# A hybrid decoder layer: the output projection as seven half-size products instead of a full product

## The chip, the cores and the metric

One core of one Trainium2 chip runs the kernel. The metric is the device time of one execution in microseconds (us); three runs of the kernel before took 1262.02, 1262.72 and 1263.93, with a median of 1262.72.

## The reference, cut to what is computed

One layer over 1024 tokens of width 1024, all in float32:

```python
h = rmsnorm(x, norm_g)
proj = h @ w_in                       # q, k, v, gates, decay code, merge logits
...
y_a = o_gla @ w_pa                    # o_gla: chunked gated linear attention (4 heads)
y_b = o_sb @ w_pb                     # o_sb: stick-breaking attention (8 heads)
gates = sigmoid(m_logits + b_gate)
merged = gates[:, :, 0] * y_a + gates[:, :, 1] * y_b
x = x + merged @ w_o                  # 1024 x 1024 by 1024 x 1024
return rmsnorm(x, final_g)
```

The change concerns the last two lines: `merged @ w_o`, the residual and the final norm, and also the places where their operands are prepared.

## The kernel before

Every float32 operand of a product is held as two parts: a high part that ScalarE (ACT) rounds off, and a low part, the difference, that VectorE (DVE) computes (`split`, L152 to 154). A product of two such operands is three matmuls: high by high, high by low and low by high. Tokens are halved (n = 0, 1 with 512 tokens each) and the rows of a weight are taken as even and odd blocks of 128 (`kb % 2`), so an activation such as `mq[n, e]` is a "quarter": 128 partitions, 4 blocks, 512 tokens.

The stages in time: the norm of x and its transposes (eight token blocks, about the first 40 us); the decay code of the linear attention, with sums of quarters of h on GpSimd (POOL); the input projection, whose products are made by `pair_job` (L233) with seven half-size products in place of eight; the two attentions; the w_pa and then the w_pb product; and the output projection.

In the w_pb stage, `m_half` (L988 on) takes each product of 512 tokens, loads the gate `d_gb` and the other branch `d_ma` into a staging tile `o`, forms the merged value and splits it into its quarter of `mq`. `Line` is the helper that issues these units beside the products. Some DMA queues matter: SP issues almost all DMAs, in program order, and one that waits holds all behind it. The engine orders are made by a scheduler, except inside `manual_schedule`, where ACT and DVE run in the order in which the code is written.

In the output projection (L1003 to L1048), the first 256 columns of w_o (`wsA`) are multiplied for all eight token blocks first, with the residual columns in `xA`; meanwhile the other 768 columns are loaded and split (`wB`). Then each token block has one bank of 512 columns and one of 256. `finish` adds the residual (DVE), squares with a running sum (ACT, `ssq`) and multiplies with the final norm's weight `fg` (DVE). When all three column parts of a block are in, DVE makes `pre` and `r`, POOL raises `r` to the power -1/2, and DVE and ACT scale the row; SP and ACT store it. `raw` (two buffers) and `tt` (one buffer) are 4 KB-a-partition staging tiles for loaded weights; `ev` holds the tiles `f`.

Of the kernel before, what the change touches and what calls it, by code (L numbers as in the profile page):

```python
# [94 lines left out]
def hybrid_layer(ctx: ExitStack, tc: tile.TileContext, x, norm_g, w_in, w_up, b_dec,  # L95
# [30 lines left out]
    d_ogl = dram_set("ogl", GLA_H, [P, 2, T])  # L126
    d_ga, d_gb, d_ma = (dram_set(nm, KB, [P, T]) for nm in ("ga", "gb", "ma"))
    d_a21 = dram_set("a21", 2, [P, 4, HALF])

    ident = const.tile([P, P], F32, tag="ident", name="ident")  # L130
    make_identity(nc, ident)
# [8 lines left out]
    nhalf = const.tile([P, 1], F32, tag="nhalf", name="nhalf")  # L140
# [11 lines left out]
    def split(src, hi, lo, eng=nc.vector):  # L152
        nc.scalar.activation(hi, src, AF.Copy)  # L153
        eng.tensor_sub(lo, src, hi.bitcast(F32))  # L154
# [42 lines left out]
    def proj_n(ws, quads, tb, n=DV):  # L197

        pt = ps.tile([P, HALF], F32, tag="pp", name="pp", bufs=3)
        cs = slice(tb % 4 * P, (tb % 4 + 1) * P)  # L200
        for kb in range(KB):
            q = quads[tb // 4, kb % 2]
            h_, l_ = q[0][:, kb // 2, cs], q[1][:, kb // 2, cs]
            whi, wlo = ws(kb)
            nc.tensor.matmul(pt[:, 0:n], h_, whi, start=kb == 0, stop=False)  # L205
            nc.tensor.matmul(pt[:, 0:n], h_, wlo, start=False, stop=False)  # L206
            nc.tensor.matmul(pt[:, 0:n], l_, whi, start=False, stop=kb == KB - 1)  # L207
# [311 lines left out]
    f = {}  # L519
# [11 lines left out]
    def part(nm, j):  # L531
# [17 lines left out]
    manual = ExitStack()  # L549
# [3 lines left out]
    st.run(1)  # L553
    for i, s in enumerate("hl"):
        nc.sync.dma_start(d_a21[i], hq[1, 0][i].bitcast(F32))
    for fn, hs in ((code, ((0,), (1,))), (logit, ((0, 1), (2, 3))), (decay_a, ((0, 1), (2, 3))),
                   (decay_b, ((0,), (1,), (2,), (3,))), (decay_c, ((0,), (1,), (2,), (3,))),
                   (decay_d, ((0,), (1,), (2,), (3,))), (decay_e, ((0, 1, 2, 3),))):
        for group in hs:
            for h in group:  # L560
                fn(h)
            st.run(1)
    for ops in line:
        for op in ops:
            op()
        st.run(1)
# [214 lines left out]
    a21b = ctx.enter_context(tc.tile_pool(name="a21b", bufs=1, side="right", reuse_waits="tile"))  # L781
# [173 lines left out]


    pq = ctx.enter_context(tc.tile_pool(name="pq", bufs=1, reuse_waits="tile"))
    pb_ctx = ExitStack()
# [5 lines left out]
    mq = {}  # L964
# [19 lines left out]
    reload_split(bq, 3, 3)  # L984
    pb_load(1)[0]()
    st.run()
    mq.update(quads_in(a21b, "m"))

    def m_half(pt, eb, n):
        o = stage().bitcast(F32)  # L990
        nc.sync.dma_start(o[:, 0], d_gb[eb][:, half(n)])
        nc.sync.dma_start(o[:, 1], d_ma[eb][:, half(n)])
        nc.vector.tensor_mul(o[:, 0], pt, o[:, 0])
        nc.vector.tensor_add(o[:, 0], o[:, 0], o[:, 1])
        q = mq[n, eb % 2]
        split(o[:, 0], q[0][:, eb // 2], q[1][:, eb // 2])

    line = []
    for eb in range(KB):
        line += ([pb_load(eb + 2)] if eb + 2 < KB else []) + [pb_unit(eb, 0), pb_unit(eb, 1)]  # L1000
    Line(line).run()

    wsA = rows_of(load_w256(w_o, 0))  # L1003
    fg = pq.tile([P, D], F32, tag="fg", name="fg", bufs=1)
    nc.sync.dma_start(fg, final_g.partition_broadcast(P))
    xA = pq.tile([P, NT, DV], F32, tag="xA", name="xA", bufs=1)
    nc.sync.dma_start(xA, x2[:, 0:DV].rearrange("(b p) c -> p b c", p=P))
    ssq = pq.tile([P, NT, 3], F32, tag="ssq", name="ssq", bufs=1)
    pb_ctx.close()
    po = ctx.enter_context(tc.tile_pool(name="po", bufs=2, side="right", reuse_waits="tile"))  # L1010
    wB = [[po.tile([P, D - DV], F32R, tag=f"wo{s}{k}", name=f"wo{s}{k}", bufs=1) for k in range(KB)]
          for s in "hl"]
    ygA = po.tile([P, NT, DV], F32, tag="ygA", name="ygA", bufs=1)
    for kb in range(KB):
        raw = raw_tile().rearrange("p a b -> p (a b)")[:, 0:D - DV]
        nc.sync.dma_start(raw, w_o[kb * P:(kb + 1) * P, DV:D])
        split(raw, wB[0][kb], wB[1][kb])

    def finish(tb, k, c0, pt, y, yg):

        n = y.shape[-1]
        nc.vector.tensor_add(y, pt, y)
        junk = ps.tile([P, HALF], F32, tag="tr", name="junk")
        nc.scalar.activation(junk[:, 0:n], y, AF.Square, accum_out=ssq[:, tb, k:k + 1])
        nc.vector.tensor_mul(yg, y, fg[:, c0:c0 + n])

    for tb in range(NT):
        finish(tb, 0, 0, proj_n(wsA, mq, tb), xA[:, tb], ygA[:, tb])
    for tb in range(NT):
        ts = slice(tb * P, (tb + 1) * P)  # L1030
        y = po.tile([P, D - DV], F32, tag="y", name="y")
        nc.sync.dma_start(y, x2[ts, DV:D])
        yg = po.tile([P, D], F32, tag="yg", name="yg")
        nc.gpsimd.tensor_copy(yg[:, 0:DV], ygA[:, tb])
        for k, (c0, n) in ((1, (DV, HALF)), (2, (DV + HALF, DV))):
            a = c0 - DV
            pt = proj_n(lambda kb: (wB[0][kb][:, a:a + n], wB[1][kb][:, a:a + n]), mq, tb, n)
            finish(tb, k, c0, pt, y[:, a:a + n], yg[:, c0:c0 + n])
        pre = po.tile([P, 1], F32, tag="pre", name="pre")
        nc.vector.tensor_scalar(pre, ssq[:, tb, 0:1], ssq[:, tb, 1:2], D * EPS, op0=ALU.add, op1=ALU.add)  # L1040
        r = po.tile([P, 1], F32, tag="r", name="r")
        nc.vector.tensor_scalar(r, ssq[:, tb, 2:3], pre, 1.0 / D, op0=ALU.add, op1=ALU.mult)
        nc.gpsimd.tensor_tensor(r, r, nhalf, op=ALU.pow)
        cut = 640
        nc.vector.tensor_scalar(yg[:, 0:cut], yg[:, 0:cut], r, None, op0=ALU.mult)
        nc.sync.dma_start(o2[ts, 0:cut], yg[:, 0:cut])
        nc.scalar.activation(yg[:, cut:D], yg[:, cut:D], AF.Copy, scale=r)
        nc.scalar.dma_start(o2[ts, cut:D], yg[:, cut:D])  # L1048


_INS = ["x", "norm_g", "w_in", "w_dec_up", "b_dec", "gla_norm_g", "w_pa", "w_pb", "b_gate",
# [20 lines left out]
```

## Time and profile before

| | us |
|---|---|
| median of three runs | 1262.72 |
| the profiled execution, its own time | 1259.98 |
| its span, from the first to the last instruction | 1258.3 |
| TensorE busy | 1234.0 |
| VectorE (DVE) busy | 753.4 |
| ScalarE (ACT) busy | 519.8 |
| GpSimd (POOL) busy | 243.3 |

The profile is one execution, recorded instruction by instruction. PE is TensorE, SP the engine that issues DMAs; "SPq" marks a DMA issue, with the time that the issue took. A row of the timeline gives the start in us from the span's start, the duration, the engine, the line of the kernel, the operation, out<-in and, in brackets, how long the engine stood idle before it and what ended that. A row of groups gives a count, busy time and mean ns of one, and then idle time before them with its releasers. Rows of windows give the length, then the busy time of PE, weight loads, DVE, ACT and POOL with their counts, the granted clock, the share of the DMA engines and the GB/s. Matmuls are pipelined: the time of one is the distance between two starts, not the printed duration.

### The profile page before, as it was taken

Reading aid. Unit: us, or ns where it says so; the run is one execution under the profiler, and the core shown is the slowest. Engines: PE = TensorE matmul, PEld = TensorE weight load, DVE = VectorE, ACT = ScalarE, POOL = GpSimd, SP = SyncE. Lnnn points to the kernel's source line nnn. Section 1 sums busy time; section 2 is a strip of 40 time slices with the busy share of each in tenths; the row PEclk is TensorE's granted clock in tenths of the full one; section 3 lists DMA queues with packets and bytes.
Section 4 is the critical chain, followed back from the end, with each engine's and each line's share of the span. In section 5 each row is a group of like instructions: output and inputs, shape, how many; then the busy total and the mean of one; then the engine's idle time right before and its main releaser. Section 6 shows DMA issues by size and latency. Waiting matters only on the chain.

```text
span 1258.3 us, 18805 instructions
## 1 busy us (share of the span) xinstructions
PE 1234.0 (98%) x6947; PEld 1054.5 (84%) x6947; DVE 753.4 (60%) x1309; ACT 519.8 (41%) x1024; POOL 243.3 (19%) x280
## 2 busy tenths in 40 slices
PE   8999999999999999999999999999999999999998
PEld 8999999888888888888888877777777878888986
DVE  5682454545667666666564357778887775444533
ACT  5454332344344444444444444545644443122322
POOL 2400471323223233232323010000100000000010
PEclk9999999999999999999999999999999999999999
DMA  7547353534644565655433765444775437543232
GB/s 270 186 142 269 126 181 133 188 116 149 192 157 137 188 208 173 215 179 177 159 117 121 246 206 160 135 163 147 220 245 175 135 109 265 190 161 110 85 116 92
DMA packets 176982, 212.09 MB, mean 169 GB/s; under 512 B 11222, under 2 KB 129004, under 8 KB 174332
## 3 DMA queue, kind: packets, MB, share of 16 engines
q1 hardware_dynamic: 175740, 209.34, 50.8%
q10 hardware_dynamic: 1152, 1.57, 0.3%
q8 instruction: 54, 0.88, 0.3%
q14 instruction: 36, 0.29, 0.1%
HBM read 133.28 MB, written 77.59 MB: 168 GB/s over the span
## 4 chain that ended last, share of the span: by engine, by line
PE 84%; DVE 8%; DMA 3%; ACT 2%; issue 2%; SPq 0%; POOL 0%; DVEq 0%; POOLq 0%; ACTq 0%
PE pp L254 12%; PE pp L256 12%; PE pp L255 12%; PE pp L207 7%; PE pp L205 7%; PE pp L206 7%; PE pp L193 6%; PE pp L194 6%; PE pp L192 5%; DVE eb L828 3%; PE av L864 1%; DVE be L833 1%; PE tr L847 1%; PE av L865 1%; PE av L863 1%
## 5 line engine op out<-in xcount | busy, mean ns | idle before, releaser
L153 ACT ACTIVATE wh<-raw 128x1024 fp32r<-128x1024 f32 x57 | 60.4, 1060 | 125.8 <-PE pp L193 69.6
L154 DVE TENSOR_TENSOR wl<-tt,wh 128x1024 fp32r<-128x1024 f32 x48 | 58.8, 1224 | 69.3 <-ACT wh L153 69.1
L291 DVE TENSOR_TENSOR f<-pp,f 128x512 f32<-128x512 f32 x72 | 49.7, 690 | 81.2 <-PE pp L256 77.9
L154 DVE TENSOR_TENSOR wl<-raw,wh 128x1024 fp32r<-128x1024 f32 x57 | 78.2, 1371 | 29.4 <-ACT wh L153 28.4
L153 ACT ACTIVATE wh<-tt 128x1024 fp32r<-128x1024 f32 x48 | 50.9, 1061 | 75.7 <-PE pp L255 69.0
L830 POOL TENSOR_SCALAR_AFFINE_SELECT be<-be 128x128 f32<-128x128 f32 x64 | 23.0, 360 | 277.1 <-ACT be L822 211.1
L828 DVE TENSOR_TENSOR_SCAN eb<-eb 128x128 f32<-128x128 f32 (+6 forms) x56 | 71.8, 1282 | 5.6 <-ACT eb L821 3.1
L154 DVE TENSOR_TENSOR o<-pp,o 128x256 fp32r<-128x256 f32 (+1 forms) x72 | 32.4, 451 | 66.1 <-ACT o L153 63.0
L153 ACT ACTIVATE o<-pp 128x256 fp32r<-128x256 f32 (+1 forms) x72 | 29.0, 403 | 93.5 <-PE pp L207 90.3
L821 ACT ACTIVATE eb<-z 128x384 f32<-128x384 f32 (+4 forms) x96 | 48.4, 506 | 44.6 <-PE z L819 30.7
L260 ACT ACTIVATE f<-pp 128x512 f32<-128x512 f32 x72 | 42.5, 590 | 55.8 <-PE pp L256 55.8
L228 POOL TENSOR_TENSOR tt<-raw 128x512 f32<-128x512 f32 x24 | 31.2, 1302 | 150.4 <-DVE wl L154 135.8
L153 ACT ACTIVATE ath<-tr 128x512 fp32r<-128x512 f32 (+2 forms) x96 | 44.0, 496 | 38.8 <-PE tr L847 37.9
L215 POOL TENSOR_TENSOR r<-r,nhalf 128x1 f32<-128x1 f32 x40 | 23.4, 586 | 188.3 <-DVE r L214 188.3
L154 DVE TENSOR_TENSOR atl<-tr,ath 128x512 fp32r<-128x512 f32 (+2 forms) x96 | 51.1, 546 | 5.3 <-ACT ath L153 5.3
L864 PE MATMUL av<-atl,v 128*128 128x256 f32 x160 | 47.0, 293 | 3.9 <-DVE atl L154 3.9
L847 PE MATMUL tr<-ident,be 128*128 128x128 f32 x288 | 44.5, 278 | 5.8 <-DVE be L833 4.9
L847 PEld LDWEIGHTS tr<-ident,be 128*128 128x128 f32 x288 | 32.5, 140 | 20.7 <-DVE be L833 11.2
L192 PE MATMUL pp<-bh,wh 128*128 128x512 f32 x128 | 49.9, 390 | 0.0
L193 PE MATMUL pp<-bl,wh 128*128 128x512 f32 x128 | 49.9, 390 | 0.0
L194 PE MATMUL pp<-bh,wl 128*128 128x512 f32 x128 | 49.9, 390 | 0.0
L833 DVE TENSOR_TENSOR be<-be,eb 128x128 f32<-128x128 f32 (+3 forms) x64 | 48.3, 755 | 1.9
(406 smaller groups left out, 4177.2 us busy)
## 6 DMA issues: line engine op xcount, KB each, us to landing
raw<-in_w_in_dram SPq DMA_DIRECT2D x31, 1024.0 KB, 5.9
d_v<-o SPq DMA_DIRECT2D x32, 256.0 KB, 3.2
d_gv<-o SPq DMA_DIRECT2D x16, 512.0 KB, 2.7
v<-d_gv SPq DMA_DIRECT2D x32, 256.0 KB, 3.1
d_q<-o SPq DMA_DIRECT2D x16, 512.0 KB, 5.7
d_k<-o SPq DMA_DIRECT2D x16, 512.0 KB, 3.9
k<-d_k SPq DMA_DIRECT2D x8, 1024.0 KB, 5.0
v<-d_v SPq DMA_DIRECT2D x8, 1024.0 KB, 6.6
```

The costliest lines, as they stand in the source:

```text
L153: nc.scalar.activation(hi, src, AF.Copy)
L154: eng.tensor_sub(lo, src, hi.bitcast(F32))
L192: nc.tensor.matmul(pt, whi[:, kb], h_, start=kb == 0, stop=False)
L193: nc.tensor.matmul(pt, whi[:, kb], l_, start=False, stop=False)
L194: nc.tensor.matmul(pt, wlo[:, kb], h_, start=False, stop=kb == KB - 1)
L205: nc.tensor.matmul(pt[:, 0:n], h_, whi, start=kb == 0, stop=False)
L206: nc.tensor.matmul(pt[:, 0:n], h_, wlo, start=False, stop=False)
L254: nc.tensor.matmul(pt, bh[:, j], ah[:, j], start=first and j == 0, stop=False, skip_group_check=True)
L255: nc.tensor.matmul(pt, bh[:, j], al[:, j], start=False, stop=False, skip_group_check=True)
L256: nc.tensor.matmul(pt, bl[:, j], ah[:, j], start=False, stop=j == 3, skip_group_check=True)
L828: nc.vector.tensor_tensor_scan(rest, rest, rest, om[:, T - P:T - P + 1], op0=ALU.mult, op1=ALU.min)
L847: nc.tensor.transpose(pt[:, b * P:(b + 1) * P], be[:, c:c + P], ident)
```

## The change

The output projection becomes 28 products: seven half-size products u = 0 to 6, each for four blocks t of 128 tokens of either half. Sums of quarters of w_o (T1 to T4) and of the merged activation (S1 to S4) are formed on POOL, and written to DRAM until they are read back and split.

```
T1 = w12 - w11   T2 = w22 - T1   T3 = w22 - w12   T4 = w21 - T2
S1 = m21 + m22   S2 = S1 - m11   S4 = m12 - S2    S3 = m11 - m21
```

Here the first index of m is the token half and the second the even or odd row blocks; the first of w (`b[e][J]` in the code) is the even or odd row blocks and the second the column half. So product u has the operands (A11, B11), (A12, B21), (S2, T2), (S1, T1), (S4, B22), (S3, T3), (A22, T4). Two products at most share a bank of PSUM: u = 0, 2, 5 and 6 accumulate in the four banks `xb`; u = 1 has a `pp` bank of its own; u = 3 has a `pp` bank in which u = 4 goes on.

The early sums of w_o: four jobs load 1 MB each into `tt`, take four sums and store four times, spread over the units of the decay section.

```diff
+    def t_load(j):
+        wt[j] = sw.tile([P, 4, 4, P], F32, tag="tt", name="tt", bufs=1).rearrange("p q a c -> p q (a c)")
+        for two in range(2):
+            nc.sync.dma_start(wt[j][:, 2 * two:2 * two + 2],
+                              w_o[(2 * j + two) * P:(2 * j + two + 1) * P].rearrange("p (h c) -> p h c", h=2))
+    def t_sums(j):
+        a = wt[j]
+        for dst, x1, x2_ in ((0, 1, 0), (1, 3, 1), (3, 3, 0), (2, 2, 3)):
+            nc.gpsimd.tensor_sub(a[:, dst], a[:, x1], a[:, x2_])
+    def t_store(j):
+        for i, nm in enumerate(("T1", "T3", "T4", "T2")):
+            nc.sync.dma_start(d_t[nm][j // 2][:, j % 2], wt[j][:, i])
+    for j in range(4):
+        for at, fn in ((0, t_load), (2, t_sums), (4, t_store)):
+            tjobs[5 * j + at] = lambda fn=fn, j=j: fn(j)
```

In the w_pb stage `m_half` writes a tile `m`, and splits only those of the first token half (A11, A12); the order of the last units becomes (6, 0), (7, 0), (6, 1), (7, 1). After each four units come four POOL sums, and one unit later their stores:

```diff
+        m = ms[j, n, e] = mo.tile([P, HALF], F32, tag="m", name="m")
         nc.vector.tensor_mul(o[:, 0], pt, o[:, 0])
-        nc.vector.tensor_add(o[:, 0], o[:, 0], o[:, 1])
-        q = mq[n, eb % 2]
-        split(o[:, 0], q[0][:, eb // 2], q[1][:, eb // 2])
+        nc.vector.tensor_add(m, o[:, 0], o[:, 1])
+        if n == 0:
+            hi, lo = op[("A11", "A12")[e]]
+            split(m, hi[:, j], lo[:, j])
...
+    for t in range(4):
+        y_load(0, t)
+    for t in range(3):
+        y_load(1, t)
+    m_stores(3)[0]()
+    o_load("S2")[0]()
```

The last stage runs ACT and DVE by hand in this order: item k of `items` is multiplied, then what `ev_at` names is evicted, then the loads and splits of `prep[k]`:

```diff
+        elif u == 3:
+            add(1, t, 1, zb[t])
+        elif u == 4:
+            add(0, t, 1, zb.pop(t))
+            square(0, t, 1)
+            scale(0, t, slice(0, D))
+            put(0, t, nc.sync, slice(0, D))
+        elif u == 5:
+            add(1, t, 1, xb[t])
+            square(1, t, 1)
+            nc.vector.tensor_mul(ys[1, t][:, half(1)], ys[1, t][:, half(1)], fg[:, half(1)])
...
+    items = ([(u, t) for u in range(3) for t in range(4)] + [(u, t) for t in range(4) for u in (3, 4)] +
+             [(u, t) for u in (5, 6) for t in range(4)])
+    ev_at = {0: [], 1: [0], 2: [1, 2]}
+    prep = {0: [o_part("T2", 0)], 1: [o_part("T2", 1), o_load("S1")], 3: [o_part("S2", 0)],
+            4: [o_part("S2", 1), o_load("B22")],
...
+    for k, it in enumerate(items):
+        item(*it)
+        for e in ev_at.get(k, [k]):
+            evict(*items[e])
+        Line(prep.get(k, [])).run()
```

`add` is a DVE add of a bank of 512 columns to the residual row block `y`, `square` an ACT square with its running sum and then DVE's `pre` or `r` with POOL's power, `scale` a DVE multiplication with `r` and `fg`, `o_part` a split of half an operand (128 x 1024) on ACT and DVE. The first four adds have nothing to wait for but their bank and `y`.

Three places in the engines' orders follow; in the changed kernel the lines before the new code count three more. First POOL, from the norm of the token blocks on, where `r` is a power of the norm, `tt` a sum of w_o, `f` a sum of h quarters, and `wst`, `rst` tiles of the decay code. Before:

```order
L215 TENSOR_TENSOR r<-r,nhalf 128x1 [waits DVE_49] x2
L215 TENSOR_TENSOR r<-r,nhalf 128x1 [waits DVE_49,Pool_49] x5
L526 TENSOR_TENSOR f<-ha21h,ha21l 128x512 [waits DVE_49]
L526 TENSOR_TENSOR f<-ha22h,ha22l 128x512 [waits DVE_49]
L529 TENSOR_TENSOR f<-f 128x512 [waits Pool_49]
L526 TENSOR_TENSOR f<-ha11h,ha11l 128x512
L468 MEMSET rst 128x1024 [waits PE_49]
L467 MEMSET wst 128x512 [waits PE_49]
```

After, on the same engine at the same place:

```order
L218 TENSOR_TENSOR r<-r,nhalf 128x1 [waits DVE_49,Pool_49] x3
L554 TENSOR_TENSOR tt<-tt 128x512 [waits DMAHW4_49]
L554 TENSOR_TENSOR tt<-tt 128x512 [waits DMAHW5_49,Pool_49]
L554 TENSOR_TENSOR tt<-tt 128x512 [waits Pool_49] x2
L218 TENSOR_TENSOR r<-r,nhalf 128x1 [waits DVE_49] x2
L554 TENSOR_TENSOR tt<-tt 128x512 [waits DMAHW4_49,DMAHW6_49,DMAHW3_49,DMAHW7_49,DMAHW2_49,Pool_49]
L529 TENSOR_TENSOR f<-ha21h,ha21l 128x512 [waits DVE_49]
L529 TENSOR_TENSOR f<-ha22h,ha22l 128x512 [waits DVE_49]
L554 TENSOR_TENSOR tt<-tt 128x512 [waits DMAHW5_49,Pool_49]
L532 TENSOR_TENSOR f<-f 128x512 [waits Pool_49]
L554 TENSOR_TENSOR tt<-tt 128x512 [waits Pool_49]
L470 MEMSET wst 128x512 [waits PE_49]
```

Four sums of w_o stand ahead of the last two powers, and three more ahead of the memset of `wst`, which is itself ahead of `rst` now.

Second SP, at the end of the w_pb stage, where `d_gb` and `d_ma` are inputs of the last merged blocks, `y` a row block of the residual, `raw` a weight or operand to be split, `d_sS_179`, `_181`, `_183` and `_185` the second halves of S1, S2, S3 and S4 and `d_sA_187` that of A22. Before:

```order
L991 DMA o<-d_gb_159 128x512 [waits DMAHW1_49,DVE_49]
L992 DMA o<-d_ma_167 128x512 [waits DMAHW7_49]
L1016 DMA raw<-in_w_o_dram 128x768 [waits DMAHW0_49,DVE_49]
L1032 DMA y<-in_x_dram 128x768 [waits PE_49,Pool_49]
L1032 DMA y<-in_x_dram 128x768 [waits DMAHW2_49]
```

After, again on SP, from the same loads on:

```order
L1032 DMA o<-d_ma_167 128x512 [waits DMAHW4_49]
L1057 DMA d_sA_187<-m 128x512 [waits DMAHW5_49,DVE_49]
L1056 DMA d_sS_179<-f 128x512 [waits DMAHW6_49,Pool_49]
L1056 DMA d_sS_181<-f 128x512 [waits DMAHW7_49,Pool_49]
L1056 DMA d_sS_185<-f 128x512 [waits DMAHW0_49,Pool_49]
L1115 DMA y<-in_x_dram 128x1024 [waits DMAHW1_49,PE_49]
...
L1115 DMA y<-in_x_dram 128x1024 [waits DMAHW7_49]
L1056 DMA d_sS_183<-f 128x512 [waits DMAHW0_49]
L1076 DMA raw<-d_sS_181 128x1024 [waits DMAHW1_49]
L1076 DMA raw<-d_sS_178 128x1024 [waits DMAHW2_49,DVE_49]
```

Where w_o and two row blocks of 768 columns were loaded, three stores, seven row blocks of 1024 columns (the row of "..." stands for five of them) and one more store are issued ahead of the second half of S2.

Third DVE, within the last stage, where `pp` and `xb` are banks, `pre` and `r` the scale of a row, and `wl`, `mS3l` low parts of operands. Before, one token block:

```order
L1022 TENSOR_TENSOR y<-pp,y 128x512 [waits DMAHW1_49,PE_49]
L1025 TENSOR_TENSOR yg<-y,fg 128x512 [waits DVE_49]
L1040 TENSOR_SCALAR pre<-ssq 128x1 [waits Activation_49]
L1022 TENSOR_TENSOR y<-pp,y 128x256 [waits PE_49]
L1025 TENSOR_TENSOR yg<-y,fg 128x256 [waits DVE_49]
L1042 TENSOR_SCALAR r<-ssq,pre 128x1 [waits Activation_49]
L1045 TENSOR_SCALAR yg<-yg,r 128x640 [waits Pool_49]
```

After, from the first product of u = 3 on:

```order
L1141 TENSOR_TENSOR y<-pp,y 128x512 [waits PE_49]
L157 TENSOR_TENSOR wl<-raw,wh 128x1024 [waits DMAHW0_49,Activation_49]
L1141 TENSOR_TENSOR y<-pp,y 128x512 [waits DVE_49,PE_49]
L1153 TENSOR_SCALAR pre<-ssq,pre 128x1 [waits Activation_49]
L1162 SCALAR_TENSOR_TENSOR y<-y,pre,fg 128x1024 [waits Pool_49]
L1141 TENSOR_TENSOR y<-pp,y 128x512
L157 TENSOR_TENSOR wl<-raw,wh 128x1024 [waits DMAHW1_49,Activation_49]
L157 TENSOR_TENSOR mS3l<-raw,mS3h 128x1024 [waits DMAHW2_49,Activation_49]
```

Between two adds of banks DVE has splits of later operands, and the scaling of a finished row, which waits for POOL, stands ahead of the next add.

More of the change, by code (lines that the diff above doesn't have):

```diff
@@ L561, in hybrid_layer @@
                 fn(h)
+            tjobs.pop(at, int)()
+            at += 1
             st.run(1)
+    for job in tjobs.values():
+        job()
     for ops in line:
@@ L962, in b_dma @@
         reload_dma((d_osb[2 * j], d_osb[2 * j + 1]), j)
-    mq = {}
     def pb_load(eb):
@@ L1013, in hybrid_layer @@
[L1013 to L1048, printed above, removed]
@@ new lines, in product @@
+    def product(bank, a, b, t, first):
+        (ah, al), w = op[a], op[b]
+        cs = slice(t * P, (t + 1) * P)
+        for j in range(4):
+            bh, bl = (v[:, j % 2] for v in w[j // 2]) if isinstance(w, list) else (v[:, j] for v in w)
+            nc.tensor.matmul(bank, ah[:, j, cs], bh, start=first and j == 0, stop=False, skip_group_check=True)
+            nc.tensor.matmul(bank, ah[:, j, cs], bl, start=False, stop=False, skip_group_check=True)
+            nc.tensor.matmul(bank, al[:, j, cs], bh, start=False, stop=j == 3, skip_group_check=True)
@@ new lines, in fresh_bank, with add, square @@
+    def fresh_bank():
+        return ps.tile([P, HALF], F32, tag="pp", name="pp", bufs=3)
+    def add(n, t, J, bank):
+        y = ys[n, t][:, half(J)]
+        nc.vector.tensor_add(y, bank, y)
+    def square(n, t, J):
+        i = n * 4 + t
+        junk = ps.tile([P, HALF], F32, tag="av", name="junk", bufs=1)
+        nc.scalar.activation(junk, ys[n, t][:, half(J)], AF.Square, accum_out=ssq[:, i, J:J + 1])
+        if (n, t) not in pre:
+            pre[n, t] = py.tile([P, 2], F32, tag="pre", name="pre", bufs=8)
+            nc.vector.tensor_scalar(pre[n, t][:, 0:1], ssq[:, i, J:J + 1], D * EPS, None, op0=ALU.add)
+        else:
+            r = pre[n, t][:, 1:2]
+            nc.vector.tensor_scalar(r, ssq[:, i, J:J + 1], pre[n, t][:, 0:1], 1.0 / D, op0=ALU.add, op1=ALU.mult)
+            nc.gpsimd.tensor_tensor(r, r, nhalf, op=ALU.pow)
@@ new lines, in item, with place, t3 @@
+    def item(u, t):
+        if u in (1, 3):
+            zb[t] = fresh_bank()
+        bank = zb[t] if u in (1, 3, 4) else xb[t]
+        product(bank, *(("A11", "B11"), ("A12", "B21"), ("S2", "T2"), ("S1", "T1"), ("S4", "B22"), ("S3", "T3"),
+                        ("A22", "T4"))[u], t, u in (0, 1, 3))
+    def place(nm, tile_):
+        return (lambda: op.__setitem__(nm, tile_()), False)
+    def t3():
+        return [tuple(sw.tile([P, KB, P], F32R, tag=tag, name=tag).rearrange("p k c -> p (k c)")
+                      .rearrange("p (j c) -> p j c", j=2) for tag in ("wh", "wl")) for _ in range(2)]
```

121 lines of the change are left out of this document (109 added, 12 removed).

## The prediction

> **What bounds the kernel now.** First the page's span, busy times, chain and clock, to see which engine sets the end.
>
> ```profile
> span 1258.3 us, 18805 instructions
> PE 1234.0 (98%) x6947; PEld 1054.5 (84%) x6947; DVE 753.4 (60%) x1309; ACT 519.8 (41%) x1024; POOL 243.3 (19%) x280
> PEclk9999999999999999999999999999999999999999
> PE 84%; DVE 8%; DMA 3%; ACT 2%; issue 2%; SPq 0%; POOL 0%; DVEq 0%; POOLq 0%; ACTq 0%
> ```
>
> TensorE is busy for 98% of the span at full clock and has 84% of the chain: a matmul taken away counts, if nothing else becomes late. Next the timeline of PE about the last stage (start, duration, engine, line).
>
> ```profile
> 1161.19 0.39 PE L194 MATMUL pp<-bh,wl 128*128 128x512 f32 x1
> 1161.42 0.28 PE L205 MATMUL pp<-wh,ma11h 128*128 128x256 f32 x1
> ...
> 1235.10 0.39 PE L205 MATMUL pp<-woh,ma21h 128*128 128x512 f32 x1
> ...
> 1240.44 0.39 PE L207 MATMUL pp<-woh,ma22l 128*128 128x512 f32 x1
> 1251.85 0.28 PE L207 MATMUL pp<-woh,ma22l 128*128 128x256 f32 x1
> ```
>
> The output projection starts at 1161.42, called t0 below, directly behind the last w_pb product, and its last matmul starts at 1251.85: about 90.55 us of PE without a hole. From t0 to the end of the span are 96.9 us. Rows 1235.10 to 1240.44 are 24 matmuls of 512 columns, so one takes 5.34/23 = 0.2325 us. Last, what follows PE at the end:
>
> ```profile
> 1249.31 0.69 DVE L1022 TENSOR_TENSOR y<-pp,y 128x512 f32<-128x512 f32 x1 [3.10 <-PE pp L207]
> 1250.04 0.60 ACT L1024 ACTIVATE junk<-y 128x512 f32<-128x512 f32 x1 [3.77 <-DVE y L1022]
> 1250.58 0.19 ACT L1024 ACTIVATION_READ_ACCUMULATOR junk<-y 128x1 f32 x1
> 1253.16 0.21 DVE L1042 TENSOR_SCALAR r<-ssq,pre 128x1 f32<-128x1 f32 x1
> 1253.52 0.55 POOL L1043 TENSOR_TENSOR r<-r,nhalf 128x1 f32<-128x1 f32 x1 [7.90 <-DVE r L1042]
> 1254.10 0.55 DVE L1045 TENSOR_SCALAR yg<-yg,r 128x640 f32<-128x640 f32 x1 [0.73 <-POOL r L1043]
> 1254.68 0.33 SPq L1046 DMA_DIRECT2D out_dram<-yg  x1
> ```
>
> This is the unit of the new stage: DVE add 0.69, ACT square 0.73 (1250.04 to 1250.77), DVE r 0.21, a 0.15 step to POOL's power of 0.55, the scaling, with steps of 0.02 to 0.04 between. The end comes 3.6 us after the last DMA's issue.
>
> **The change, part by part.** *Products.* 28 products of 12 matmuls of 512 columns are 336 x 0.2325 = 78.1 us, where 90.55 were: 12.4 us less on PE alone. Whether the end follows depends on DVE and ACT, which run in the hand-written order of the diff. DVE gets 28 adds, 20 splits and the scaling, and each instruction holds up all behind it.
>
> *Early sums of w_o.* The first 512 KB loads of w_o queue on SP behind the first d_v store; their sums on POOL stand ahead of the powers of token blocks 6 and 7.
>
> ```profile
> 23.12 17.21 SPq L333 DMA_DIRECT2D d_v<-o  x6
> raw<-in_w_in_dram SPq DMA_DIRECT2D x10, 512.0 KB, 4.3
> 27.86 0.55 POOL L215 TENSOR_TENSOR r<-r,nhalf 128x1 f32<-128x1 f32 x1 [3.93 <-DVE r L214]
> 31.83 0.55 POOL L215 TENSOR_TENSOR r<-r,nhalf 128x1 f32<-128x1 f32 x1 [3.43 <-DVE r L214]
> 33.86 1.28 DVE L374 SCALAR_TENSOR_TENSOR xs<-xt,r,gb 128x1024 f32<-128x1024 f32 x1
> 35.28 1.06 PE L393 MATMUL tr<-ident,xs 128*128 128x128 f32 x8
> 52.95 1.29 POOL L529 TENSOR_TENSOR f<-f 128x512 f32<-128x512 f32 x1
> 54.32 1.29 POOL L526 TENSOR_TENSOR f<-ha21h,ha21l 128x512 f32<-128x512 f32 x1
> ```
>
> Issued at about 24, landed 4.3 later, the first sum starts at 28.4, just behind block 5's power. Four, 1.37 apart (52.95 to 54.32), end near 33.8; block 6's power then ends at 34.4 where it ended at 32.38. The norm that reads it began at 33.86, so its slack of 1.5 is used up and DVE, then the transposes of 35.28, come 0.5 late or more. A DVE instruction beside a POOL sum can also be slower:
>
> ```profile
> 254.31 2.10 DVE L154 TENSOR_TENSOR wl<-raw,wh 128x1024 fp32r<-128x1024 f32 x1 [0.15 <-ACT wh L153]
> 1097.07 0.69 DVE L994 TENSOR_TENSOR o<-o 128x512 f32<-128x512 f32 x1
> 1097.67 1.22 DVE L154 TENSOR_TENSOR wl<-raw,wh 128x1024 fp32r<-128x1024 f32 x1
> 1098.81 0.69 DVE L154 TENSOR_TENSOR ma22l<-o,ma22h 128x512 fp32r<-128x512 f32 x1
> PE pp L205 <- DVE o L154: 0.2, 1, 0.2
> ```
>
> The split took 2.10 at 254.31, beside a POOL sum, and 1.22 at 1097.67, where POOL is idle: 0.88 more. Bounds for this part: 0 (the loads land after block 7's power, or PE has the work to cover it) and 4 x 0.88 = 3.5. PE waits only 0.2 in 40 to 215 (last row), so what it loses early it doesn't get back. I take **+1.0**, near the 0.5. The later sums lie between POOL's own sums. The memset of `wst` moves behind three of them, and ahead of one of POOL's old sums and of the `rst` memset:
>
> ```profile
> 46.37 0.95 POOL L468 MEMSET rst<- 128x1024 f32 x1
> 47.26 0.52 POOL L467 MEMSET wst<- 128x512 f32 x1
> 50.19 1.28 ACT L479 ACTIVATE wst<-wup 16x512 fp32r<-16x512 f32 x2 [0.58 <-DMA wup<-in_w_dec_up_dram]
> ```
>
> That is 3 x 1.29 - 1.29 - 0.89 (46.37 to 47.26) = 1.7 later, ending at 49.5 ahead of its reader at 50.19: nothing, and up to 1 if POOL is a little behind. The twelve later stores and loads ride on SP among others whose results are needed only tens of us later; nothing for them.
>
> *The w_pb stage.* The m sums (POOL) and m stores (SP) run beside products of 5.4 us; four sums are 5.3. SP waits for them, but the loads of d_gb and d_ma go out over a unit ahead: nothing, bounds 0 and 1.
>
> *From t0 to the second half of S2.* This is the first operand that is late. The last m is ready at t0+1.6 (0.20 of drain to the row of 1161.62, 0.73 and 0.69), and POOL's S1, S2 and S4, 1.37 apart, end at 5.8. SP stores them as they come; then it issues seven y loads of 512 KB, the S3 store, and only then S2's second half: 4.45 MB with it.
>
> ```profile
> 1161.62 0.69 DVE L993 TENSOR_TENSOR o<-pp,o 128x512 f32<-128x512 f32 x1 [2.63 <-PE pp L194]
> 1160.98 0.81 SPq L1032 DMA_DIRECT2D y<-in_x_dram  x2
> 4.00:8.00 4.00, 2.74 (x16) 2.54 (x15) 1.44 (x2) 1.15 (x3) 0.55 (x1) 1.00 1.04 347
> ...
> 12.00:16.00 4.00, 3.15 (x26) 2.96 (x26) 2.25 (x4) 1.55 (x5) 1.10 (x2) 1.00 1.02 419
> y<-in_x_dram SPq DMA_DIRECT2D x8, 384.0 KB, 3.0
> GB/s 270 186 142 269 126 181 133 188 116 149 192 157 137 188 208 173 215 179 177 159 117 121 246 206 160 135 163 147 220 245 175 135 109 265 190 161 110 85 116 92
> ```
>
> In the two windows of four us the DMA share is full (1.04, 1.02) at 347 and 419 GB/s (last number). At 400 the 4.45 MB take 11.1. One issue takes 0.4 (0.81 for two). Of a DMA's time to landing 2.0 to 3.0 are not transfer (384 KB: 3.0 less 1.0; 512 KB: 4.3 less 1.3); I take 2.7. From S4 at 5.8, then, S2 lands at 5.8 + 0.4 + 11.1 + 2.7 = **t0+20.0**. By 419 it is 10.6 and by 347 it is 12.8, so -0.5 to +1.7; the page's slices, means of 31 us, have 270 at most, which is the far end (rival 2). *A rule that speaks against 400:* the Trainium skill, DMA: Bandwidth & Descriptors, "Where 436 GB/s comes from", gives about 358 GB/s as what one core gets from HBM, and 435 as the fabric's ceiling. By 358, as an estimate, the burst takes 12.4 and the sum below rises by 1.3. The trace has 419 GB/s in a window of mixed loads and stores, so the row doesn't hold to the lower figure.
>
> *From S2 on,* DVE's order sets the pace. Two durations more:
>
> ```profile
> L153 ACT ACTIVATE wh<-raw 128x1024 fp32r<-128x1024 f32 x9 | 9.6, 1062 | 36.7 <-PE pp L193 30.4 <-DMA o<-d_gb 6.4
> L504 DVE SCALAR_TENSOR_TENSOR e<-u,e 128x1024 f32<-128x1024 f32 x4 | 4.9, 1218 | 1.9 <-ACT e L503 1.9
> ```
>
> Back to back, DVE starts the next 0.60 behind a 512-wide one and 1.14 behind a 1024-wide one (rows of 1097.07 to 1098.81). Then:
> - split of S2's second half, ACT 1.06 + 0.03 + DVE 1.22: t0+22.3.
> - three rounds of add 0.69, 0.02, square 0.73, ACT split 1.06, 0.03, DVE split 1.14 = 3.66: 33.3. The square holds the next split on ACT.
> - four adds and five splits without a wait, 4 x 0.60 + 5 x 1.14 = 8.1: 41.4.
> - four rounds of u = 3 and 4. The product of u = 4 writes on in the bank of u = 3, so it waits for the add that reads it: 0.72 for add and hop, 12 x 0.2325 = 2.79, drain 0.20, then add 0.69, 0.02, square 0.73, 0.03, r 0.21, 0.15, power 0.55, 0.03, scaling 1.22 less 0.08 of overlap. Together 7.26, four times: 29.0, 70.4. The next add stands behind the scaling on DVE, though its product has long been done.
> - u = 5: 3.67 with A22's last split, then 3 x 2.25 (add, square, pre, product with fg): 10.4, 80.8.
> - u = 6: add 0.69, square 0.73, r 0.21, power 0.55, scaling 0.69 and 0.14 of steps = 3.01, four times: 12.0, 92.8.
> - the last DMA: 3.65: **t0+96.5**, where 96.9 was: **-0.4**.
>
> So PE's 12.4 us become holes: its products stand still behind the rounds. The sum is +1.0 - 0.4 = **+0.6 us**: 1260.6 for the profiled execution (1259.98 with 1.7 outside its span), and 1262.72 + 0.6 = **1263.3** against the median of the three runs.
>
> **Rivals.** *1, faster: PE sets the end.* Were DVE's and ACT's waits hidden, the last product would end at 78.1, and 0.2 + 3.0 + 3.65 behind it give t0+85.0: -11.9, with +1.0 the time is **1251.8**. For it: DVE's work itself is 28 adds (0.69), 20 splits and 4 scalings (1.22), 8 more of 0.69 and 16 of 0.21 = 57.5, within 78. Against: the work is in order, and each square, r and power round stands between two adds. An earlier S2 alone gains 2.5 at most, as DVE is free only at about t0+17.5: 1260.8. Chance of it all 0.08.
>
> *2, slower: the y burst.* The seven y loads go ahead of S2's second half, so at 269 GB/s, the page's second highest slice, 4.45 MB take 16.5: 5.4 more. It decides from S2's landing after about t0+20: each us there is a us at the end, as nothing on DVE can go ahead. **1268.7**, chance 0.2. The longest hole of PE in my sum is 2.2 us, and in this rival it passes 3; the trace of before has a clock of nine tenths or more in every slice and shows no such hole. The Trainium skill, TensorE: Matmul & The Clock Gate, "Why this matters for your kernels", says that a hole of over about 3 us lets the clock fall to half; a product behind it would take up to 2.8 longer, beside DVE's rounds, and no run here shows it yet.
>
> *3, slower: the early sums.* All of 3.5 in place of 1.0: **1265.8**, chance 0.15. DVE's rows in 28 to 34 would be longer.
>
> *4, the product count brings nothing,* as 512 columns in the new order run slower than 0.2325 each. For no change it needs the order to be PE-bound, which it isn't; it would be seen and not felt (0.02).
>
> **How the numbers follow.** 1263.3 has 0.5: DVE's order, S2 at about 20, early +1. The remaining 0.05 are for an earlier S2. A measurement of this kernel tells about 0.2% (2.5 us) from no change. Faster by that, under 1260.2: rival 1, half of the early S2 cases and part of the forecast with early 0: 0.15. Same: most of the forecast, some of rival 3: 0.5. Slower, over 1265.2: rivals 2 and 3 and the upper end of the forecast: 0.35. The range goes from 1260 (early 0 and an early S2) to 1270 (rival 2 and a little of 3); rival 1 is left out.
>
> **What would show it.** In the profile after: PE's busy sum from t0 near 78 with holes of 0.5 to 2.2 before the u = 4 and u = 6 products; S2's second half landing at t0+20; DVE's rounds at 3.66, 7.26, 2.25 and 3.01; the transposes of block 6 about 1 later than 35.28. It is wrong if PE has no holes in the stage (rival 1), if S2 lands after 22 (rival 2), or if the w_pb stage starts several us late (rival 3).

## The result: 0.7% slower, and the profile after

The changed kernel takes 1270.56 us (median of 4 runs, 1270.07 to 1272.89) where the kernel before takes 1262.41 (4 runs, 1262.02 to 1263.93): 1.0066 times as long, with a 95% interval of 1.0049 to 1.0083, or 8.15 us more. The prediction was 1263.3 with a range of 1260 to 1270; the time lies just above it. The profiled execution after took 1270.07.

The head of the page of the changed kernel:

```profile
span 1268.3 us, 18415 instructions
PE 1224.9 (97%) x6707; PEld 1034.6 (82%) x6707; DVE 773.7 (61%) x1299; ACT 525.4 (41%) x1010; POOL 293.4 (23%) x304
```

PE has lost 9.1 us of busy time and the span has grown by 10.0. To see where, the same instructions are matched in both timelines and the later start is read off, called the shift below. It is 0.06 at 20 us, 2.3 at 36, 5.4 from 100 to 740, and 7.67 where the last stage begins (1169.09 for 1161.42). The stage itself takes 99.2 where it took 96.9.

The early part first: POOL, DVE and then the first eviction behind the decay section, in the timeline of the changed kernel.

```profile
29.35 6.26 POOL L554 TENSOR_TENSOR tt<-tt 128x512 f32<-128x512 f32 x4 [0.89 <-DMA tt<-in_w_o_dram]
...
35.56 0.55 POOL L218 TENSOR_TENSOR r<-r,nhalf 128x1 f32<-128x1 f32 x1
...
36.15 1.28 DVE L377 SCALAR_TENSOR_TENSOR xs<-xt,r,gb 128x1024 f32<-128x1024 f32 x1 [1.69 <-POOL r L218]
...
67.38 7.25 POOL L554 TENSOR_TENSOR tt<-tt 128x512 f32<-128x512 f32 x4 [5.09 <-DMA tt<-in_w_o_dram]
...
67.56 4.56 DVE L502 SCALAR_TENSOR_TENSOR e<-u 128x1024 f32<-128x1024 f32 x2
...
73.51 0.42 DVE L157 TENSOR_TENSOR o<-pp,o 128x256 fp32r<-128x256 f32 x1 [1.39 <-ACT o L156]
...
87.69 8.42 POOL L554 TENSOR_TENSOR tt<-tt 128x512 f32<-128x512 f32 x3 [3.23 <-DMA tt<-in_w_o_dram]
...
91.64 3.38 DVE L510 TENSOR_TENSOR_SCAN u<-rmask,e 128x1024 f32<-128x1024 f32 x1
...
106.24 0.42 DVE L157 TENSOR_TENSOR o<-pp,o 128x256 fp32r<-128x256 f32 x1 [2.43 <-ACT o L156]
```

And the rows of the kernel before that answer to those of 67.56, 91.64 and 106.24:

```profile
65.25 2.35 DVE L499 SCALAR_TENSOR_TENSOR e<-u 128x1024 f32<-128x1024 f32 x2
...
85.63 2.28 DVE L507 TENSOR_TENSOR_SCAN u<-rmask,e 128x1024 f32<-128x1024 f32 x1
...
100.82 0.42 DVE L154 TENSOR_TENSOR o<-pp,o 128x256 fp32r<-128x256 f32 x1 [2.18 <-ACT o L153]
```

Two things are to be seen. Job 0's four sums took 6.26 us, and block 6's power and norm stand behind them: the norm starts at 36.15 for 33.86. Later, jobs 2 and 3 stand beside DVE's decay work, and both slow down: the pair of L502 takes 4.56 for 2.35, a scan 3.38 for 2.28, and three POOL sums 8.42. The group of all 16 sums (count, busy time, mean ns, idle before):

```profile
L554 POOL TENSOR_TENSOR tt<-tt 128x512 f32<-128x512 f32 x16 | 29.1, 1816 | 21.7 <-DMA tt<-in_w_o_dram 21.1
```

One takes 1.82 us on average, not 1.29. Then the last stage of the changed kernel: the last w_pb product, S2's split and the ends of the rounds in the timeline, and what PE waited for.

```profile
1168.86 0.39 PE L197 MATMUL pp<-bh,wl 128*128 128x512 f32 x1
...
1190.72 1.06 ACT L156 ACTIVATE mS2h<-raw 128x1024 fp32r<-128x1024 f32 x1 [2.40 <-DMA raw<-d_sS]
...
1204.08 0.68 DVE L1141 TENSOR_TENSOR y<-xb,y 128x512 f32<-128x512 f32 x1
...
1212.14 0.68 DVE L1141 TENSOR_TENSOR y<-pp,y 128x512 f32<-128x512 f32 x1
...
1241.97 0.68 DVE L1141 TENSOR_TENSOR y<-xb,y 128x512 f32<-128x512 f32 x1
...
1252.20 0.68 DVE L1141 TENSOR_TENSOR y<-xb,y 128x512 f32<-128x512 f32 x1
...
1264.41 0.37 ACTq L1158 DMA_DIRECT2D out_dram<-y  x1
```

```profile
PE xb L1132 <- DVE y L1141: 2.2, 1, 2.2
...
PE pp L1132 <- DVE y L1141: 2.2, 5, 0.8
```

```profile
sum 99.21, PE 79.74 PEld 61.94 DVE 55.45 ACT 31.89 POOL 10.47; mean PE 79.74 PEld 61.94 DVE 55.45 ACT 31.89 POOL 10.47
```

Against the steps of the prediction, in us after t0 (1168.86 + 0.23 = 1169.09):

| step | predicted | measured |
|---|---|---|
| split of S2's second half begins | 20.0 | 21.6 |
| three rounds of u = 1 end | 33.3 | 35.0 |
| first add of u = 3 | 41.4 | 43.1 |
| rounds of u = 3 and 4 end | 70.4 | 72.9 |
| u = 5 ends | 80.8 | 83.1 |
| end of the span | 96.5 | 99.2 |
| PE's busy sum | 78.1 | 79.7 |

PE is busy for 79.7 of the 99.2 us, where it was 90.7 of 96.9: the eighth of the products was saved. Of the 19.5 us without PE, 6.3 are holes between products, and 13.2 follow the last product, where DVE's rounds go on alone (6.2 in the kernel before, with no hole). So the saved time went about half into holes and half into a longer end, both behind DVE's order.

### The profile page after: what moved, and what is told of

It is laid out like the page before. It is cut to its first block, busy times and chain, and to the rows that moved or that the text cites. A ratio compares the mean times of both kernels' runs of the same rounds, so it can differ in the third digit from the quotient of the medians.

```text
span 1268.3 us, 18415 instructions
## 1 busy us (share of the span) xinstructions
PE 1224.9 (97%) x6707; PEld 1034.6 (82%) x6707; DVE 773.7 (61%) x1299; ACT 525.4 (41%) x1010; POOL 293.4 (23%) x304
```

## Experiments

Each kernel's profile is one execution; "shift" is against the first profile of the kernel before, "S2 split" the time from t0 at which ACT begins the split of S2's second half, "stage" the time from t0 to the end of the span. Times are of one run unless said otherwise; the runs of one kernel lie up to 4.5 us apart (nine of e8_best, 1255.84 to 1260.35), so a single time settles little, and the argument rests on the timelines.

| run | what differs | time | shift at 100 to 210 | t0 | S2 split | stage |
|---|---|---|---|---|---|---|
| before, first profile | | 1259.98 | 0 | 1161.42 | | 96.9 |
| e0_before | before, again | 1261.93 | 0 | 1163.37 | | 96.8 |
| changed kernel | | 1270.07 | 5.4 | 1169.09 | 21.6 | 99.2 |
| e1_no_tsums | without T sums | 1268.31 | -0.2 | 1166.13 | 22.9 | 100.5 |
| e2_before_plus_t | before, with T jobs | 1268.84 | 5.0 | 1169.97 | | 97.1 |
| e11_no_sums23 | without sums 2, 3 | 1270.00 | 2.1 | 1168.47 | 21.9 | 99.6 |
| e3_s2_first | S2 ahead of all y | 1273.26 | 5.1 | 1171.41 | 22.2 | 100.2 |
| e7_ysplit | S2 ahead of three y | 1271.68 | 5.4 | 1170.10 | 20.6 | 99.9 |
| e4_skew2 | order of ACT, DVE | 1259.41 | 5.5 | 1171.46 | 22.7 | 86.1 |
| e5_late | T jobs later | 1273.61 | 1.0, then 6.2 | 1170.88 | 23.3 | 100.9 |
| e10_late2 | T jobs at other steps | 1269.44 | 2.6 | 1167.20 | 22.9 | 100.5 |
| e8_best | e5, e7 and e4 | 1258.10 (9 runs) | 6.0 | 1169.79 | 18.7 | 84.7 |
| e9_best2 | e10, e7 and e4 | 1254.73 (5 runs) | 2.6 | 1169.97 | 19.2 | 84.7 |

**Is it the sums, or their traffic?** In e1_no_tsums the sums are left out, so T isn't the sum of w_o's quarters; in e2_before_plus_t the jobs are put into the kernel before.

```diff
-        for at, fn in ((0, t_load), (2, t_sums), (4, t_store)):
+        for at, fn in ((0, t_load), (4, t_store)):
```

> The sums T1 to T4 on POOL are left out; the loads of w_o and the four stores a job stay, so what is read back as T is not the sum. The changed kernel reaches its last stage 7.67 us later than the kernel before (1169.09 for 1161.42): 5.42 of it by 100 us, 2.25 between 740 and 935 us. Theory 1 (the POOL sums themselves: they hold the powers of the norm and slow DVE beside them): block 6's norm is back at 33.9 to 34.0, DVE's L502 pair back at 2.35 for 4.56, and at 100 us the shift is 0 to 0.6. Theory 2 (the traffic of the T loads and stores, 8.4 MB on the same queue): 3 to 5.5 us of shift at 100 us stay. For the 2.25 in the attention: if the new instruction order there causes it, it stays; if it is the luck of one execution, it is anything between 0 and 2.5. Time 1263.5 to 1267 by theory 1, 1268 to 1271 by theory 2.

> The kernel before, with the T loads, sums and stores of the decay section added and nothing else changed; what they write is not used. Theory 1 (POOL sums beside DVE and ahead of the powers): shift of 5 to 6 us at 100 us, and the same at the end: 1267 to 1269. Theory 2 (traffic) says the same time, so it is e1 that parts them; this run shows if the early part alone carries the loss, and what the attention section does with the old order and an early shift: 0 to 0.5 more if its 2.25 came with the new order, up to 2 if it follows the shift or is luck.

The eviction of 106.24 in the timeline of e1_no_tsums:

```profile
100.66 0.42 DVE L157 TENSOR_TENSOR o<-pp,o 128x256 fp32r<-128x256 f32 x1 [2.17 <-ACT o L156]
```

It is at 100.66, a shift of -0.2, with all 8.4 MB of traffic still there; e2 has 5.0 with the sums and everything else as before. The early loss is the POOL sums; standing there, the traffic costs nothing. The time of e1 (1268.31) doesn't show this: it lies in the range of theory 2, as its attention section took 4.9 us longer than in the first profile of the kernel before and its stage 3.6. Both are taken up below.

**What do jobs 0 and 1 cost, and what jobs 2 and 3?** e11_no_sums23 leaves out the sums of the latter, so half of T isn't the sum.

```diff
-            tjobs[5 * j + at] = lambda fn=fn, j=j: fn(j)
+            if fn is not t_sums or j < 2:
+                tjobs[5 * j + at] = lambda fn=fn, j=j: fn(j)
```

> The sums of the T jobs 2 and 3 are left out (their loads and stores stay); those of jobs 0 and 1 stand where they were. By the rows of the changed kernel, jobs 0 and 1 hold the powers and slow one norm (2.3 us by 36 us), and jobs 2 and 3 slow DVE's decay work (3.1 more by 100 us). If that division holds: shift 2.2 to 2.6 at 60 us and at 120 us. If the traffic of loads and stores or the held powers make the later part too, the shift grows to 4 or more by 120 us.

The same eviction in e11_no_sums23:

```profile
102.92 0.42 DVE L157 TENSOR_TENSOR o<-pp,o 128x256 fp32r<-128x256 f32 x1 [2.18 <-ACT o L156]
```

102.92 is a shift of 2.1, a little under the 2.2 to 2.6 that were expected, and it doesn't grow between 60 and 340 us. Jobs 0 and 1, with the held power of block 6, make 2.1 to 2.3, and the sums of jobs 2 and 3, beside which the rows above show DVE slower, the other 3.1 to 3.3.

**Does S2's landing hold the stage?** e3_s2_first issues the last stores and S2's load ahead of all seven y loads, e7_ysplit ahead of the three of the second token half.

```diff
     for t in range(4):
         y_load(0, t)
-    for t in range(3):
-        y_load(1, t)
     m_stores(3)[0]()
     o_load("S2")[0]()
+    for t in range(3):
+        y_load(1, t)
```

> The stores of the last S sums and the load of S2's second half are issued ahead of the seven y loads. In the changed kernel ACT starts the split of S2's second half at t0+21.6 and the stage takes 99.2. If S2's landing alone holds the stage: ACT starts it at t0+18 to 19, limited by DVE's order, and the stage is 96.5 to 97.5. Rival (the y loads are then what is late: DVE's first adds wait for them instead): the split starts at 20 to 22 and the stage stays at 98.5 to 99.5. Early part as in the changed kernel (7 to 8 us later at the last stage, or 5.4 if the attention's part was luck).

> The three y loads of the second token half, which are needed only at t0+43, go behind S2's second half; the four of the first half stay ahead of it. In the changed kernel the split of S2 starts at t0+21.6 and the stage takes 99.2. If each us of S2's landing costs one at the end until DVE is free at t0+19.4: split at 19.4 to 19.8, stage 96.9 to 97.5. Rival (something else holds the stage, or loads of S1 and T1 are then late): 98.5 to 99.5.

Both missed. In e3 the rival was right in kind: the four y that the first adds need came later, S2's split began at t0+22.2, and the stage took 100.2. In e7 the split began at 20.6, 1.0 earlier, and the first add of u = 3 came at 42.0 for 43.1; but the stage didn't get shorter. Its PE timeline and a window of it (length, PE, PEld, DVE, ACT, POOL, clock, DMA share, GB/s):

```profile
1212.97 0.61 PE L1132 MATMUL pp<-wB22h,mS4h 128*128 128x512 f32 x1 [3.10 <-DVE y L1141]
```

```profile
1210.10:1215.10 5.00, 2.13 (x6) 1.68 (x7) 3.86 (x5) 0.48 (x1) 0.00 (x0) 0.80 0.95 327
```

With S2 earlier PE ran ahead, then stood for 3.10 us at the first product of u = 4, which waits for DVE's add; behind that hole the clock was down and a matmul took 0.61. From the add of u = 3 to that of u = 4 it is 5.4 us instead of 3.9. So 1.0 won at S2 was lost again, with some 0.6 more, at the next place where DVE's order holds PE. The rest of the table shows what S2's landing is worth in the other direction. The changed kernel, e11, e1, e10 and e5 have the same last stage, and in these executions S2 lands at different times: the split begins at 21.6, 21.9, 22.9, 22.9 and 23.3, and the stage takes 99.2, 99.6, 100.5, 100.5 and 100.9. From the split to the end it is 77.6 in all five, and 79.2 in e7.

**Is it DVE's order that keeps PE's gain?** e4_skew2 changes only the order of ACT and DVE in the last stage, and with it POOL's powers: the square of u = 1, and `pre`, `r`, the power and the scaling of a row, come an item or two later, and for items 5 to 7 the split stands ahead of the eviction.

```diff
         elif u == 4:
             add(0, t, 1, zb.pop(t))
             square(0, t, 1)
-            scale(0, t, slice(0, D))
-            put(0, t, nc.sync, slice(0, D))
+            later(fin)
+            rs.append(lambda: (first(0, t, 0), rstd(0, t, 1)))
+            fin.append(lambda: (scale(0, t, slice(0, D)), put(0, t, nc.sync, slice(0, D))))
```

> Only the hand-written order of ACT and DVE in the last stage is changed: squares, r, the power and the scaling of a row come one item later, and for items 5 to 7 the split stands ahead of the eviction, so no DVE instruction waits for a round through ACT and POOL. Theory (DVE's in-order rounds, 3.6, 7.4, 2.2 and 3.0 us each, are what keeps PE's 12 us from the end): the stage falls from 99.2 to 85 to 88, PE's holes vanish but for 1 to 2 us, and PE's busy sum stays at 78 to 79. Rival (DVE's amount of work, or the landing of operands one buffer behind, is the limit): the stage stays above 93.

PE's waits in the last stage of e4_skew2, and the sum of the window over the stage:

```profile
PE pp L1132 <- DVE y L1141: 1.2, 2, 0.8
...
PE xb L1134 <- DVE mS2l L157: 0.5, 1, 0.5
```

```profile
sum 86.14, PE 77.47 PEld 62.42 DVE 54.62 ACT 31.47 POOL 12.31; mean PE 77.47 PEld 62.42 DVE 54.62 ACT 31.47 POOL 12.31
```

The stage takes 86.1 for 99.2 with the same DVE work (54.6 and 55.5), though S2's split begins at 22.7. DVE's amount of work was never the limit; where it stood in line was. With an early part that still costs 5.5 us, this kernel took 3.9 less than the kernel before on the same chip (1263.34, one run each).

**Can the sums stand somewhere else?** e5_late and e10_late2 take the T jobs out of the decay section, to steps of the 36 behind it, with POOL in written order there.

```diff
-    manual.enter_context(tc.manual_schedule(engines={mybir.EngineType.Activation, mybir.EngineType.DVE}))
+    manual.enter_context(tc.manual_schedule(engines={mybir.EngineType.Activation, mybir.EngineType.DVE,
+                                                     mybir.EngineType.Pool}))
...
-            tjobs.pop(at, int)()
-            at += 1
...
+    for at, ops in enumerate(line):
         for op in ops:
             op()
+        tjobs.pop(at, int)()
         st.run(1)
```

> The changed kernel with the four T jobs moved out of the decay section into the 36 steps behind it, and POOL held to the written order there, so that no T sum stands ahead of a power of the norm or beside DVE's 1024-wide decay work. If the 5.42 us of the early part come from those two, the shift at 120 us falls to 0 to 1, and the time to 1264.5 to 1267. If the sums cost the same wherever they stand (POOL's time, or traffic), the shift at 200 us is 3 to 5.5 and the time 1268 to 1271.

> All three: T jobs late with POOL in written order, y loads of the second half behind S2, and the order of ACT and DVE that never waits for its own round. Early shift 0 to 1, stage 84 to 86.5 (PE-bound: 28 x 12 x 0.2325 = 78.1, then 0.2 + 3.0 + 3.6) where before has 96.9: 1250 to 1253 against 1262.4 for the kernel before, 0.990 to 0.993 of it. If either the T sums cost the same wherever they stand, or the stage doesn't get under 90, it is 1256 to 1260.

The early part was back at 1.0 up to 170 us, and then 4.7 us came at one place, between 202 and 206 us. POOL's timeline of e8_best, which has the same jobs, and a window behind that place:

```profile
189.03 5.74 POOL L554 TENSOR_TENSOR tt<-tt 128x512 f32<-128x512 f32 x4
...
198.89 1.29 POOL L231 TENSOR_TENSOR tt<-raw 128x512 f32<-128x512 f32 x1 [4.12 <-DMA d_tT<-tt]
```

```profile
205.00:210.00 5.00, 4.50 (x25) 4.50 (x26) 2.31 (x6) 0.62 (x2) 0.00 (x0) 0.66 0.93 318
```

Job 3 had the one `tt` buffer until its store was through at 198.9, while the input projection's first pair wants it (164 us in the kernel before); ACT and DVE stood behind it in written order, PE waited 3.0 us, and behind that hole its clock was 0.66. So e5_late missed its time. e8_best as a whole is 0.9968 of the kernel before (0.9958 to 0.9978), at 1258.10, in the range that was given for sums that cost the same wherever they stand, and above the 1250 to 1253 that were expected. Moved to the 8th, 10th, 16th and 21st step:

> The changed kernel with only the T jobs moved as in e9_best2; the last stage is that of the changed kernel. This undoes the early part alone: shift at 210 us 0 to 1.5 where the changed kernel has 5.4, stage 98.5 to 101, time 1264 to 1268.

> As e8_best, with the T jobs at other steps behind the decay section (after the 8th, 10th, 16th and 21st of its 36), so that the last is done by about 175 us, ahead of the input projection's first use of the one `tt` buffer, for which PE waited 3.0 us at about 200 us in e8_best; job 0 stands beside DVE work that reads PSUM. Shift at 60 us 0 to 0.3 (0.9 in e8_best), at 210 us 0 to 1.5 (6.0 there), stage 84 to 86: median 1251 to 1255, 0.991 to 0.995 of the kernel before. If the sums cost 5 us wherever they stand: 1257 to 1260.

At 210 us the shift is 2.6 in both, better than 6.0 and more than the 0 to 1.5 expected. It comes at one place, where PE waits 1.5 us for an eviction that stands behind a split. SP issues the four stores of job 3 between 160.1 and 164.8, and the load for that split only behind them, at 165.35 where it was 158.03. ACT's split in e9_best2, and in the kernel before:

```profile
172.45 0.63 ACT L156 ACTIVATE dh<-raw 128x512 fp32r<-128x512 f32 x1 [7.43 <-DMA raw<-in_w_in_dram]
```

```profile
164.01 0.63 ACT L153 ACTIVATE dh<-raw 128x512 fp32r<-128x512 f32 x1 [2.73 <-DMA raw<-in_w_in_dram]
```

By these timelines the stores do cost something here, through their place in SP's order; no run takes them out. e10_late2's time is 1.4 above its range; its stage (100.5) is within what was expected, its shift is 1.1 over, and its attention section took 3.2 more than in the first profile of the kernel before. **e9_best2 takes 1254.73 us, 0.9936 of the kernel before (0.9922 to 0.9949): 7.8 us faster than before and 15.8 faster than the change as it was.** Against the kernel before, e9 gains 3.8 us on e8; the two have the same stage, and their shifts at 210 us differ by 3.4, which fits an early loss that reaches the end. Their stage of 84.7 us is close to what PE needs; in e9 PE waits 0.7 us in it:

```profile
sum 84.73, PE 77.15 PEld 62.57 DVE 54.79 ACT 31.47 POOL 13.14; mean PE 77.15 PEld 62.57 DVE 54.79 ACT 31.47 POOL 13.14
```

**The attention section.** Between 740 and 945 us the code computes the same in all kernels, yet the shift grows there by 2.25 in the changed kernel.

> The kernel before once more, for a second profile. The first profile of it (1259.98) is 2.4 us under the median of its other runs (1262.4), and the attention section between 735 and 945 us differs by -0.5 to +5 us among kernels whose code there is the same. Theory (the length of that section is the luck of an execution: when w_pa's blocks land, and if PE's clock falls behind the hole that they leave): this profile is 1 to 4 us longer there than the first, without any change of the code. Rival (the early T traffic and the new order there make it longer): the section takes the same time as in the first profile, within 0.5 us.

The second profile of the kernel before is 1.95 us longer than the first, 1.55 of it at one place, about 932 us. In the others the growth was 2.3 to 6.0 us (4.9 in e1, 3.6 in e2, 6.0 in e9). So an execution of the same kernel can differ by nearly the 2.25. That fits the medians: 5.4 of the early part and 2.3 of the stage make 7.7 of the 8.15 without this section. But every profile of a kernel with the T loads and stores, e1 without the sums and e2 with the old last stage too, grew more here than either profile of the kernel before. Whether one or two us of that section come with the change stays open.

## Why the prediction was wrong

- **What bounds the kernel, and DVE's order:** right. The forecast was that PE's 12.4 us become holes; PE's busy sum fell by 11.0 (90.7 to 79.7) and the stage didn't get shorter. About half of it became holes, and the rest a longer end behind the last product. e4_skew2 shows the cause by taking it away.
- **The early sums of w_o: this step failed.** "I take +1.0, near the 0.5" measured 5.4. In kind, job 0 did what was written (its sums ahead of block 6's power, DVE beside them slower), but its first sum began at 29.35, not 28.4, and the four took 6.26, not 5.4, so the norm came 2.3 late and not 0.5. And "the later sums lie between POOL's own sums" was priced at nothing without asking what DVE does beside jobs 2 and 3, though the row of 254.31 had given the price of a DVE instruction beside a POOL sum: 0.88. Eight sums beside it cost 3.1 to 3.3. The upper bound of 3.5 counted job 0 alone, so rival 3 was too small as well. e1 and e11 part the two sizes, and the rows show how they come about. By row 67.38, the pair of L502, begun 0.18 behind job 2's first sum, takes 4.56, which is its own 2.35 and 2.21 more, somewhat under two sums of 1.29, and the four sums take 7.25, which is 5.16 and 2.09 more, somewhat under the pair. The two engines look as if they took turns. The eviction at 73.51 beside the same sums, with one input from PSUM, keeps its 0.42. The Trainium skill, SBUF — State Buffer, "Who interferes with whom", has this as a rule: a DVE instruction with two inputs in SBUF and a GpSimd instruction that reads SBUF block each other for a whole instruction, and a DVE instruction with one such input, outside the modes that use two ports, doesn't contend. These rows agree; the prediction didn't apply it.
- **S2's landing:** 1.6 late of its 20.0. The timeline of the changed kernel has a split on DVE and the first two of the last four sums on POOL, and its windows the stretch ahead of the burst and the burst (columns as above):

```profile
1170.68 1.22 DVE L157 TENSOR_TENSOR wT2l<-raw,wT2h 128x1024 fp32r<-128x1024 f32 x1
...
1170.84 2.23 POOL L1045 TENSOR_TENSOR f<-m 128x512 f32<-128x512 f32 x1 [11.70 <-DVE m L1035]
1173.14 1.29 POOL L1045 TENSOR_TENSOR f<-f,m 128x512 f32<-128x512 f32 x1
```

```profile
1173.00:1177.00 4.00, 4.00 (x19) 3.32 (x18) 0.00 (x0) 0.00 (x0) 3.84 (x4) 1.00 0.42 163
...
1181.00:1185.00 4.00, 4.00 (x20) 3.30 (x19) 2.62 (x4) 0.00 (x0) 0.00 (x0) 1.00 1.02 409
```

The first sum took 2.23 for 1.29, beside DVE's split, which has two inputs in SBUF: it is the price of the early sums again, and 0.9 of the 1.6. SP issues the burst behind the stores of these sums, and from t0+4 to t0+8 the DMA share was still 0.42. The rate in the burst was 409 GB/s, near the 400 taken. It is above the 358 of the rule weighed there. Rival 2 had the right place and a wrong reason: the burst was late more than slow. The other 0.7 isn't divided further.
- **The rounds of the walk:** 3.66 was 3.6 to 3.9, 7.26 was 7.4 to 7.5, 2.25 was 2.2, 3.01 was 3.0. These held, though the four rounds of u = 3 and 4 make 0.8 of the 2.7 by which the stage is longer than forecast. A slip without weight: 5.34/23 is 0.2322, which takes 0.1 off the 78.1.
- **Rival 2's "each us there is a us at the end"** held for a later S2, with 77.6 from the split to the end in five runs. An earlier one didn't pay: e7 won a us at S2 and lost it behind a hole at the lower clock.
- Together: -0.4 was +2.3 for the stage and +1.0 was +5.4 early, 7.7 in place of 0.6. Of the chances, "slower" had 0.35, with too small prices.

## What to carry to other kernels

A sum on POOL isn't free because POOL is idle: price it by what DVE does in the same microseconds, instruction by instruction, by who else stands in POOL's queue, and its stores by the load that stands behind them in SP's. Where an engine works in written order, look for instructions that wait for a round trip begun in the same item, since they can swallow a saving on another engine; here moving the tail of each round an item or two back brought the saving out. A buffer shared with the next stage sets a latest time for whatever borrows it.

## What the runs showed of the hardware

PE's clock fell behind holes shorter than expected, and not each time. In the last stage the first product of u = 6 stands behind the same hole in two runs: 2.22 us in the changed kernel and 2.23 in e10_late2. Windows of 5 us behind it, first of the changed kernel:

```profile
1241.00:1246.00 5.00, 2.62 (x9) 1.62 (x10) 3.95 (x6) 1.67 (x3) 0.00 (x0) 1.00 0.25 105
```

and then of e10_late2:

```profile
1242.20:1247.20 5.00, 5.00 (x15) 4.00 (x16) 3.27 (x7) 2.33 (x5) 0.00 (x0) 0.66 0.26 105
```

The clock was 1.00 in the one and 0.66 in the other. It cost the stage nothing: that of e10 is 1.3 us longer, but its S2 split began 1.3 later, and from there both take 77.6. The Trainium skill, TensorE: Matmul & The Clock Gate, "Why this matters for your kernels", puts the limit at about 3 us; the hole of 3.10 in e7_ysplit agrees, and that of 2.23 was enough here. In the attention section of e1_no_tsums a hole of 2.25 us at 892 did the same:

```profile
890.00:895.00 5.00, 3.17 (x8) 2.50 (x9) 3.64 (x8) 3.13 (x7) 1.08 (x2) 0.66 0.93 310
...
935.00:940.00 5.00, 5.00 (x19) 4.02 (x18) 4.00 (x9) 1.80 (x5) 0.29 (x1) 0.56 0.80 292
```

In the first profile of the kernel before the same windows have 1.00. In the second it fell too, though the longest waits of PE close by are 0.9 and 0.7 us; e0_before first, then the first profile:

```profile
932.00:937.00 5.00, 4.75 (x19) 3.75 (x20) 4.66 (x9) 2.89 (x6) 0.29 (x1) 0.66 1.00 346
```

```profile
932.00:937.00 5.00, 4.63 (x26) 3.59 (x25) 5.00 (x10) 2.70 (x6) 0.29 (x1) 1.00 0.94 336
```

This is the place at which 1.55 us came between the two profiles. So a part of the 0 to 6 us by which profiles differ in this section is the clock. The changed kernel's 2.25 isn't: its clock stayed at 1.00 there, and its waits are 0.3 to 0.5 us longer each.
